# Nine norms of a two-block transformer kernel: one product with a matrix of ones, a square root and a reciprocal in place of column sums, a power and a spread

## The chip, the cores and the metric

The kernel runs on one core of a Trainium2 chip. Its engines go by short names here: PE is TensorE (PEld its weight loads), ACT is ScalarE, DVE is VectorE, POOL is GpSimd, SP is SyncE. The metric is the device time of one launch in microseconds (us).

## The reference, cut to what matters

One launch runs a conformer-like block over 256 tokens of 1024 features (in-projection, convolution and retention, out-projection, feed-forward, and a gated projection of a second input, "PLE"), and then two blocks of a transformer with conditioned norms (differential attention, then neighbourhood attention, each with a SwiGLU feed-forward), over 256 tokens and, in the first of the two, 256 context tokens. All of it is float32. What the change touches is the root-mean-square norm that stands at many places:

```python
def rmsnorm(x, w):
    xf = x.astype(jnp.float32)
    y = xf * lax.rsqrt(jnp.mean(xf * xf, axis=-1, keepdims=True) + EPS)
    return (y * w.astype(jnp.float32)).astype(x.dtype)

def first_block(...):
        ...
        x = x + rmsnorm(y, mix_post_norm[i])
        h = rmsnorm(x, ffn_pre_norm[i])
        f = (silu(h @ w_ffn_gate[i]) * (h @ w_ffn_up[i])) @ w_ffn_down[i]
        x = x + rmsnorm(f, ffn_post_norm[i])
        e = sigmoid(x @ w_ple_gate[i]) * (p[i] @ w_ple_proj[i])
        x = x + rmsnorm(e, ple_post_norm[i])

def second_block(...):
    for i in range(DEPTH_2):
        ...
        xn = modulate(rmsnorm_2(h, norm_mix[i]), sh_m, sc_m)
        ...
        h = h + g_m * y
        h = h + g_f * swiglu(modulate(rmsnorm_2(h, norm_ffn[i]), sh_f, sc_f), ...)
        if not last:
            hc = hc + cg_m * yc
            hc = hc + cg_f * swiglu(modulate(rmsnorm_2(hc, norm_ffn[i]), csh_f, csc_f), ...)
    return rmsnorm_2(h, norm_final)
```

## The kernel before

**Layout.** Activations are kept transposed: 8 tiles of 128 features by 256 tokens (`h[0..7]`, and `hc[0..7]` for the context). A norm over the features is therefore a sum over the 128 partitions of a tile and over the 8 tiles. Weights stream in through SP's queue as float32 blocks `raw`; ACT rounds each to a short-mantissa part `hi` (L132, a cast), DVE takes the rest `lo` (L133, a subtraction), and PE makes each float32 product of three short ones (L171, L172, L173, started 0.12 us apart at the full clock when nothing waits). Nearly all of PE's instructions are such triples, into the PSUM banks `mm`, `s` and `o`; the tiles of activations that they read are split the same way (`x`, by ACT at L154 or L670 and DVE at L155 or L671).

**A norm.** Class `Stat` gathers the squares. For each of the 8 tiles `add` lets ACT square it (L231 for the first, into `acc`; L234 for the others, into `sq`) and DVE add the square to `acc` (L236), save for the last square, which stays apart. `rstd` then makes the scale. For `acc` and for the last `sq`, two products each with a column of ones give the 256 sums as two columns of 128 (L247, four instructions, which the trace shows as 8 records). DVE scales them and adds EPS (L217), POOL raises them to the power -0.5 (L218), and two products with the identity spread each column over the partitions again, as 128 by 256 in a PSUM bank `t` (L256, 4 records). Then DVE multiplies tiles by that bank (L560 behind out_proj and the first block's feed-forward, L667 in the conditioned norms, L757 behind PLE, L1257 in the norm "NE" of the last feed-forward, where two columns are appended), or a copy of it is made first (L263, and L1288 at the end of the program). `fill` is a pair of hooks with which a norm puts other ready products behind the column products and behind the spreading ones, so that PE has work while DVE and POOL make the scale.

**Where norms stand.** There are 14, all made with that method. Nine are touched by the change; I number them by time: 1 behind out_proj (134 us), 2 behind the first block's feed-forward (358), 3 behind PLE (419), 4 and 5 behind the out-projection of differential attention, for `h` (621) and `hc` (642), 6 and 7 behind the first feed-forward of the transformer, for `h` and `hc` (990, 1015), 8 the norm NE (1210), 9 the final norm (1390). In the final norm the outputs are already multiplied by the norm's weights (L1281), and POOL (3 tiles, L1292) and DVE (5 tiles, L1295) multiply them by the scale and issue the transfers to the output.

**What sets the order.** Each engine runs its instructions in program order. That order is chosen when the kernel is built, by a scheduler that lays out the instructions of all engines by its own estimates, with hints in the code (`tc.issue_after(x)` places what follows behind `x`). So a change in one place can also move instructions of other lines.

**Functions of ACT.** Square root, exponential, tanh and SiLU need a table loaded into ACT, and a load (an instruction of its own, ACT_TABLE_LOAD) stands ahead of an activation whenever its function is not in the table that is loaded. The kernel before has 5 loads.

## Time and profile before

| | us |
|---|---|
| median of 3 runs (lowest, highest) | 1398.66 (1398.44, 1399.48) |
| the profiled execution, its own time | 1401.17 |
| its span (first to last instruction) | 1399.4 |
| PE busy in the span | 1368.7 (98%) |
| DVE busy | 1073.0 (77%) |
| ACT busy | 696.4 (50%) |
| POOL busy | 62.1 (4%) |
| mean granted clock of PE, as a share of the full one | 0.993 |

The page gives the busy time of each engine, the chain of work that ended last, and the costliest groups of instructions. A busy PE is one with an instruction under way; the end of each product is modelled, 0.28 us behind its start, while the next one starts 0.12 us behind it, so idle time of PE is read a little short: a gap of 0.51 us in a row is 0.67 us by the starts of the products around it. The other views are the timeline (start, length, engine, line, operation, and in square brackets how long the engine was idle before it and for whom), the groups by line, one line with those that waited for it, and busy times by stretch.

### The profile page before, as it was taken

How to read it: one execution, taken by the hardware profiler on the slowest of the kernel's cores; microseconds unless marked ns; L12 is line 12 of the kernel's file. 1: busy time of each engine (PE TensorE's matmuls, PEld its weight loads, DVE VectorE, ACT ScalarE, POOL GpSimd, SP SyncE). 2: the span in 40 equal slices, each digit the busy share in tenths (PEclk: the TensorE clock that was granted, in tenths of full speed). 3: DMA queues.
4: the chain of work that ended last, by engine and by line, in shares of the span. 5: the costliest groups of instructions: out<-in, count | busy, mean ns of one | idle time of the engine just before them, and what ended most of it. 6: DMA issues, size and time to landing. Idle time of an engine off the chain costs nothing.

```text
span 1399.4 us, 24793 instructions
## 1 busy us (share of the span) xinstructions
PE 1368.7 (98%) x9465; PEld 1231.3 (88%) x9465; DVE 1073.0 (77%) x2167; ACT 696.4 (50%) x1316; POOL 62.1 (4%) x119
## 2 busy tenths in 40 slices
PE   7999999999999999999999999999999999999997
PEld 7798799999999989899888888888998888888886
DVE  7975899986678878977799999964765467798764
ACT  6656544454465777655332222323545456655442
POOL 0001000000000222310000000000000000000000
PEclk9999999999999999999999999999999999999998
DMA  8456688767455333334565676644632234355463
GB/s 294 137 167 208 225 304 293 228 201 220 161 178 176 107 113 122 106 96 154 168 213 186 219 237 224 205 132 116 200 121 95 80 91 135 124 195 185 154 187 93
DMA packets 78600, 239.76 MB, mean 171 GB/s; under 512 B 8977, under 2 KB 14609, under 8 KB 78353
## 3 DMA queue, kind: packets, MB, share of 16 engines
q1 hardware_dynamic: 77760, 237.65, 52.6%
q8 instruction: 74, 1.21, 0.3%
q10 hardware_dynamic: 720, 0.53, 0.1%
q14 instruction: 46, 0.37, 0.1%
HBM read 237.10 MB, written 1.05 MB: 170 GB/s over the span
## 4 chain that ended last, share of the span: by engine, by line
PE 91%; DVE 3%; ACT 2%; issue 1%; POOL 1%; DMA 1%; SPq 0%; POOLq 0%; DVEq 0%; ACTq 0%
PE mm L171 20%; PE mm L172 19%; PE mm L173 19%; PE mm L183 5%; PE s L183 2%; PE mm L185 2%; PE mm L198 2%; PE mm L200 2%; PE mm L199 2%; PE s L821 1%; PE s L171 1%; PE t L852 1%; PE s L172 1%; PE s L173 1%; PE s L1131 1%
## 5 line engine op out<-in xcount | busy, mean ns | idle before, releaser
L132 ACT CAST hi<-raw 128x1024 fp32r<-128x1024 f32 (+3 forms) x383 | 364.7, 956 | 504.4 <-PE mm L172 261.5
L133 DVE TENSOR_TENSOR lo<-raw,hi 128x1024 fp32r<-128x1024 f32 (+3 forms) x383 | 422.0, 1104 | 149.8 <-ACT hi L132 146.9
L171 PE MATMUL mm<-x,hi 128*128 128x256 f32 (+2 forms) x1412 | 445.1, 317 | 9.2 <-ACT x L154 6.1
L172 PE MATMUL mm<-x,hi 128*128 128x256 f32 (+2 forms) x1412 | 443.0, 314 | 2.0 <-DVE x L155 1.1
L173 PE MATMUL mm<-x,lo 128*128 128x256 f32 (+2 forms) x1412 | 442.1, 314 | 1.8 <-DVE lo L133 1.8
L171 PEld LDWEIGHTS mm<-x,hi 128*128 128x128 f32 x1412 | 270.3, 192 | 39.4 <-issue 12.2
L172 PEld LDWEIGHTS mm<-x,hi 128*128 128x128 f32 x1412 | 271.4, 192 | 20.9 <-issue 3.3
L173 PEld LDWEIGHTS mm<-x,lo 128*128 128x128 f32 x1412 | 271.4, 192 | 19.4 <-issue 2.9
L292 DVE SCALAR_TENSOR_TENSOR junk<-adaw,sb 128x512 f32<-128x512 f32 x320 | 219.9, 687 | 12.6 <-DMA adaw<-ada 8.2
L173 PE MATMUL mm<-o,lo 128*128 128x256 f32 (+1 forms) x284 | 85.0, 301 | 0.0
L172 PE MATMUL mm<-o,hi 128*128 128x256 f32 (+1 forms) x284 | 84.5, 300 | 0.0
L171 PE MATMUL mm<-o,hi 128*128 128x256 f32 (+1 forms) x284 | 83.8, 302 | 0.6 <-ACT o L150 0.5
L218 POOL TENSOR_TENSOR rv<-rv,mhalf 128x2 f32<-128x2 f32 (+1 forms) x16 | 16.5, 1032 | 1185.2 <-DVE rv L217 1185.2
L198 PE MATMUL mm<-hi,x 128*128 128x256 f32 x240 | 68.7, 286 | 0.0
L199 PE MATMUL mm<-lo,x 128*128 128x256 f32 x240 | 68.6, 286 | 0.0
L200 PE MATMUL mm<-hi,x 128*128 128x256 f32 x240 | 68.6, 286 | 0.0
L172 PE MATMUL mm<-q,hi 128*128 128x256 f32 (+1 forms) x195 | 61.1, 313 | 0.0
L171 PE MATMUL mm<-q,hi 128*128 128x256 f32 (+1 forms) x195 | 61.0, 313 | 0.0
L173 PE MATMUL mm<-q,lo 128*128 128x256 f32 (+1 forms) x195 | 61.0, 313 | 0.0
L171 PEld LDWEIGHTS mm<-o,hi 128*128 128x128 f32 x284 | 53.5, 191 | 3.8 <-ACT o L150 0.9
L173 PEld LDWEIGHTS mm<-o,lo 128*128 128x128 f32 x284 | 54.2, 191 | 2.1 <-issue 0.4
L172 PEld LDWEIGHTS mm<-o,hi 128*128 128x128 f32 x284 | 54.2, 191 | 1.8
(301 smaller groups left out, 2408.2 us busy)
## 6 DMA issues: line engine op xcount, KB each, us to landing
raw<-gu SPq DMA_DIRECT2D x88, 512.0 KB, 4.3
adaw<-ada SPq DMA_DIRECT2D x80, 512.0 KB, 4.6
raw<-wqkv SPq DMA_DIRECT2D x72, 512.0 KB, 4.3
raw<-ffn SPq DMA_DIRECT2D x44, 512.0 KB, 5.1
raw<-down SPq DMA_DIRECT2D x37, 384.0 KB, 3.1
raw<-down SPq DMA_DIRECT2D x37, 320.0 KB, 3.0
raw<-w_in SPq DMA_DIRECT2D x22, 512.0 KB, 5.5
o<-ada SPq DMA_DIRECT2D x32, 256.0 KB, 5.2
```

Source lines behind the costliest of these rows:

```text
L132: last_conv[:] = [act.copy(hi[:, :n], raw[:, :n]).ins, dve.tensor_tensor(lo[:, :n], raw[:, :n], f32(hi[:, :n]), op=ALU.subtract).ins]
L133: dve.tensor_tensor(lo[:, :n], raw[:, :n], f32(hi[:, :n]), op=ALU.subtract).ins]
L171: pe.matmul(out, wh, xh, start=first and k == 0, stop=False)
L172: pe.matmul(out, wh, xl, start=False, stop=False)
L173: last_mm[0] = pe.matmul(out, wl, xh, start=False, stop=last and k == n - 1).ins
L183: last_mm[0] = pe.matmul(out, wh, x, start=first and k == 0, stop=end).ins
L185: last_mm[0] = pe.matmul(out[:, :T], wl, x[:, :T], start=False, stop=False).ins
L198: pe.matmul(out, xh[:, ts_], wh, start=first and k == 0, stop=False)
L199: pe.matmul(out, xh[:, ts_], wl, start=False, stop=False)
L200: last_mm[0] = pe.matmul(out, xl[:, ts_], wh, start=False, stop=last and k == n - 1).ins
L218: pool.tensor_tensor(out, out, mhalf[:, :n], op=ALU.pow)
L292: dve.scalar_tensor_tensor(out=junk, in0=raw[:, gs_], scalar=1.0, in1=sb[:, v, gs_], op0=ALU.mult, op1=ALU.mult, accum_out=acc[:, n, v, g: ...
```

## The change

Nine of the 14 norms get a flag `root`. In them

- the last square is added to `acc` by DVE too (L244 of the new numbering, one more L236), save in norm 9, which has the flag `apart` and keeps it apart;
- one product of a 128 by 128 matrix of ones with `acc` (L255, 128x256, in norm 9 two: `acc` and the last square) sums over the partitions and leaves the sum in every one of them; both `fill` hooks are put behind it;
- ACT takes the square root of the bank, with scale 1/1024 and bias EPS, into `acc` in SBUF (L260), and DVE takes the reciprocal in place, 128x256 (L261);
- the result is in SBUF, not in PSUM, and the copies at L263 (norm 8) and L1288 (norm 9) go;
- behind the seventh square an activation of one column (L242) makes the table load of the square root come there, and not at L260. Functions that come after it load their own table again: there are 14 loads where there were 5.

```diff
-        def __init__(self, n, of=1024):
-            self.n, self.of, self.acc, self.left = n, of, None, of // P
+        def __init__(self, n, of=1024, root=False, apart=False):
+            self.n, self.of, self.acc, self.left, self.root, self.apart = n, of, None, of // P, root, apart or not root
...
             self.last_sq = act.activation(sq[:, :n], src, AF.Square).ins
-            if self.left:
+            if self.root and self.left == 1:
+                with tc.issue_after(self.last_sq):
+                    act.activation(first, ones[:, 0:1], AF.Sqrt)
+            if self.left or not self.apart:
                 self.last_add = dve.tensor_tensor(self.acc[:, :n], self.acc[:, :n], sq[:, :n], op=ALU.add).ins
             else:
                 self.last = sq
...
             ps = bank(pst, "t")
+            if self.root:
+                srcs = (self.acc, self.last) if self.apart else (self.acc,)
+                for src in srcs:
+                    mm = pe.matmul(ps[:, :T], ones, src, start=src is srcs[0], stop=src is srcs[-1])
+                if fill:
+                    fill[0](mm.ins)
+                    fill[1](last_mm[0])
+                r = self.acc if r is None else r[:, :T]
+                act.activation(r, ps[:, :T], AF.Sqrt, scale=1.0 / self.of, bias=eps)
+                dve.reciprocal(r, r)
+                return r
...
-    st = Stat(T)
+    st = Stat(T, root=True, apart=True)
...
     r = st.rstd(keep=False)
-    rs = tmp1()
-    act.copy(rs, r[:, :T])
     for k in (5, 0, 6, 1, 7, 2, 3, 4):
         o = outs[k // 2][:, (k % 2) * T:(k % 2 + 1) * T]
         if k > 4:
-            pool.tensor_tensor(o, o, rs, op=ALU.mult)
+            pool.tensor_tensor(o, o, r, op=ALU.mult)
```

The lines of the kernel before that stand behind the added code have numbers that are 4 to 19 higher after: L236 is L244, L560 is L579, L587 is L606, L603 is L622, L667 and L671 are L686 and L690, L1005 is L1024, L1281 is L1300.

ACT's instructions at norm 1, where the squares read out_proj's banks (`mm`), L587 copies these banks out, the casts are weights of the feed-forward, and L603 copies products of PLE. Before:

```order
L234 ACTIVATE sq<-mm 128x256 x2
L587 ACTIVATE q<-mm,vec 128x256 x2
L234 ACTIVATE sq<-mm 128x256 x2
L587 ACTIVATE q<-mm,vec 128x256 x2
L132 CAST hi<-raw 128x1024 x3
L603 ACTIVATE pt<-s 128x512
L132 CAST hi<-raw 128x1024
L603 ACTIVATE pt<-s 128x512 x2
L154 ACTIVATE x<-h_85,vec 128x256
```

After:

```order
L238 ACTIVATE sq<-mm 128x256
L242 ACT_TABLE_LOAD
L242 ACTIVATE first<-ones 128x1
L238 ACTIVATE sq<-mm 128x256
L606 ACTIVATE q<-mm,vec 128x256 x2
L132 CAST hi<-raw 128x1024 x3
L622 ACTIVATE pt<-s 128x512
L260 ACTIVATE acc<-t,eps 128x256
L132 CAST hi<-raw 128x1024
L622 ACTIVATE pt<-s 128x512 x3
```

The load and its activation stand ahead of the last square, and the square root stands behind three casts and one copy.

DVE's instructions at norm 1, up to the first multiplications by the scale (L560, which is L579 after). Before:

```order
L236 TENSOR_TENSOR acc<-acc,sq 128x256 x3
L217 TENSOR_SCALAR rv<-t 128x2
L133 TENSOR_TENSOR lo<-raw,hi 128x1024 x2
L560 TENSOR_TENSOR t_1748<-q,t 128x256
L560 TENSOR_TENSOR t_1756<-q,t 128x256
L133 TENSOR_TENSOR lo<-raw,hi 128x1024
```

After:

```order
L133 TENSOR_TENSOR lo<-raw,hi 128x1024
L244 TENSOR_TENSOR acc<-acc,sq 128x256 x4
L133 TENSOR_TENSOR lo<-raw,hi 128x1024 x3
L261 RECIPROCAL acc<-acc 128x256
L133 TENSOR_TENSOR lo<-raw,hi 128x1024
L579 TENSOR_TENSOR t_1745<-q,acc 128x256
L579 TENSOR_TENSOR t_1753<-q,acc 128x256
```

Three additions became four, the scaling of the columns is gone, and three subtractions of weights stand ahead of the reciprocal, where none stood ahead of L217; from the additions to the first multiplication there are four where there were two.

DVE's instructions at norm 5, where L1005 (L1024) adds the projection to the context tiles, L667 and L671 (L686, L690) make the tiles of norm 4's output, and the last multiplications follow. Before:

```order
L1005 SCALAR_TENSOR_TENSOR hc_96<-s,mod_108,hc_96 128x256
L133 TENSOR_TENSOR lo<-raw,hi 128x1024
L667 SCALAR_TENSOR_TENSOR t_8313<-h_91,mod_108,t 128x256
L671 SCALAR_TENSOR_TENSOR x<-t_8301,mod_108,x 128x256
L133 TENSOR_TENSOR lo<-raw,hi 128x1024
L671 SCALAR_TENSOR_TENSOR x<-t_8305,mod_108,x 128x256
L671 SCALAR_TENSOR_TENSOR x<-t_8309,mod_108,x 128x256
L217 TENSOR_SCALAR rv<-t 128x2
L667 SCALAR_TENSOR_TENSOR t_8317<-h_92,mod_108,t 128x256
```

After:

```order
L690 SCALAR_TENSOR_TENSOR x<-t_8283,mod_110,x 128x256
L686 SCALAR_TENSOR_TENSOR t_8295<-h_91,mod_110,acc 128x256
L133 TENSOR_TENSOR lo<-raw,hi 128x1024
L690 SCALAR_TENSOR_TENSOR x<-t_8287,mod_110,x 128x256
L690 SCALAR_TENSOR_TENSOR x<-t_8291,mod_110,x 128x256
L686 SCALAR_TENSOR_TENSOR t_8299<-h_92,mod_110,acc 128x256
L244 TENSOR_TENSOR acc<-acc,sq 128x256
L690 SCALAR_TENSOR_TENSOR x<-t_8295,mod_110,x 128x256
L690 SCALAR_TENSOR_TENSOR x<-t_8299,mod_110,x 128x256
L261 RECIPROCAL acc<-acc 128x256
L686 SCALAR_TENSOR_TENSOR t_8515<-hc_93,mod_110,acc 128x256
```

The last square's addition (L244) stands four instructions ahead of the reciprocal, and PE's one product of norm 5 comes between the two; before, PE's products waited for the last square only, and L217 was what stood here. On PE that product stands where the column products stood, with the triples of the next weights behind it.

ACT's instructions at the end of the program. Before:

```order
L234 ACTIVATE sq<-h_91 128x256
L1281 ACTIVATE x<-h_91,vec 128x256
L234 ACTIVATE sq<-h_92 128x256
L1281 ACTIVATE x<-h_92,vec 128x256
L1288 COPY t_15860<-t 128x256
L1293 DMA out<-x 128x256 x3
```

After:

```order
L238 ACTIVATE sq<-h_91 128x256
L242 ACT_TABLE_LOAD
L242 ACTIVATE first<-ones 128x1
L1300 ACTIVATE x<-h_91,vec 128x256
L238 ACTIVATE sq<-h_92 128x256
L1300 ACTIVATE x<-h_92,vec 128x256
L260 ACTIVATE acc<-t,eps 128x256
L1310 DMA out<-x 128x256 x3
```

The load stands behind the square of the seventh tile (`h_91`), and the square root in the place of the copy.

## Rows read from the trace of the kernel before

**Rows 1.** the page: busy time by engine, chain that ended last, and one costly group

```profile
PE 1368.7 (98%) x9465; PEld 1231.3 (88%) x9465; DVE 1073.0 (77%) x2167; ACT 696.4 (50%) x1316; POOL 62.1 (4%) x119
...
PE 91%; DVE 3%; ACT 2%; issue 1%; POOL 1%; DMA 1%; SPq 0%; POOLq 0%; DVEq 0%; ACTq 0%
...
L133 DVE TENSOR_TENSOR lo<-raw,hi 128x1024 fp32r<-128x1024 f32 (+3 forms) x383 | 422.0, 1104 | 149.8 <-ACT hi L132 146.9
```

**Rows 2.** one source line, the power on POOL (L218), and who waited for it

```profile
L218 POOL TENSOR_TENSOR rv<-rv,mhalf x16: 693/697/2069, 23.1 to 1391.3; 128x2 f32<-128x2 f32 x14, 128x4 f32<-128x4 f32 x2
...
  PE t L256: 2.6, 4
```

**Rows 3.** timeline by start time, out_proj into post_norm: start, length, engine, line, operation [idle before]

```profile
134.29 0.50 PE L247 MATMUL t<-ones,acc 128*128 128x1 f32 x4
134.31 2.96 ACT L132 CAST hi<-raw 128x1024 fp32r<-128x1024 f32 x3
...
135.11 0.36 PE L171 MATMUL s<-x,hi 128*128 128x256 f32 x1
...
135.59 1.65 POOL L218 TENSOR_TENSOR rv<-rv,mhalf 128x2 f32<-128x2 f32 x1 [25.54 <-DVE rv L217]
...
137.29 0.71 PE L256 MATMUL t<-tab,rv 128*128 128x128 f32 x4 [0.51 <-POOL rv L218]
...
137.82 0.39 PE L171 MATMUL s<-x,hi 128*128 128x256 f32 x1
...
138.04 0.75 DVE L560 TENSOR_TENSOR t<-q,t 128x256 f32<-128x256 f32 x2 [0.22 <-PE t L256]
...
142.19 0.39 PE L172 MATMUL mm<-x,hi 128*128 128x256 f32 x1 [0.82 <-DVE x L155]
```

**Rows 4.** groups of VectorE by line and shape: busy us, mean ns of one | idle before

```profile
L236 DVE TENSOR_TENSOR acc<-acc,sq 128x256 f32<-128x256 f32 x80 | 33.3, 418 | 7.8 <-ACT sq L234 6.9
...
L836 DVE RECIPROCAL sc<-sc 128x1 f32<-128x1 f32 x16 | 2.5, 158 | 6.0 <-ACT e L831 6.0
...
L836 DVE RECIPROCAL sc<-sc 128x2 f32<-128x2 f32 x8 | 1.3, 160 | 3.8 <-ACT e L831 3.8
...
L779 DVE TENSOR_SCALAR nlam<-nlam 128x1 f32<-128x1 f32 x1 | 0.1, 148 | 0.0
```

**Rows 5.** the same view of ScalarE: a table load and a one-column activation

```profile
L1083 ACT ACT_TABLE_LOAD x1 | 1.3, 1283 | 0.0
...
L110 ACT ACTIVATE first<-ones 128x1 f32<-128x1 f32 x1 | 0.2, 203 | 0.0
```

**Rows 6.** timeline: the one product with ones of this shape, and the next start

```profile
87.33 0.60 PE L439 MATMUL t<-rp,ones 128*128 128x256 f32 x2
87.76 0.59 PE L503 MATMUL s<-q 128*128 128x256 f32 x2
```

**Rows 7.** timeline around the end of the second norm behind wo0

```profile
641.60 0.42 DVE L236 TENSOR_TENSOR acc<-acc,sq 128x256 f32<-128x256 f32 x1
...
643.36 0.61 PE L247 MATMUL t<-ones,sq 128*128 128x1 f32 x4 [0.63 <-ACT sq L234]
...
646.57 0.15 DVE L217 TENSOR_SCALAR rv<-t 128x2 f32<-128x2 f32 x1
```

**Rows 8.** busy time, granted clock (behind the engines), DMA share of a ten us stretch there

```profile
640.00:650.00 10.00, 9.17 (x63) 8.91 (x63) 8.58 (x20) 4.63 (x9) 0.69 (x1) 0.83 0.83 303
```

**Rows 9.** timeline at the start of the products behind the NE norm

```profile
1216.75 0.39 PE L171 MATMUL mm<-x,hi 128*128 128x258 f32 x1 [0.50 <-DVE t L1257]
```

**Rows 10.** timeline of the last norm

```profile
1390.31 0.60 PE L247 MATMUL t<-ones,sq 128*128 128x1 f32 x4 [0.74 <-ACT sq L234]
...
1392.01 0.96 PE L256 MATMUL t<-tab,rv 128*128 128x128 f32 x4 [1.10 <-POOL rv L218]
1393.01 0.37 ACT L1288 COPY t<-t 128x256 f32<-128x256 f32 x1 [2.35 <-PE t L256]
...
1393.45 2.09 POOL L1292 TENSOR_TENSOR x<-x,t 128x256 f32<-128x256 f32 x3 [1.50 <-ACT t L1288]
```

More of the change, by code (lines that the diff above doesn't have):

```diff
@@ L212, in body @@
     dve.memset(mhalf, -0.5)
+    eps = const.tile([P, 1], F32, name="eps")
+    dve.memset(eps, EPS)
     def inv_sqrt(out, src, scale):
```

12 lines of the change are left out of this document (6 added, 6 removed).

## The prediction, made before the changed kernel ran

> **What bounds the kernel now.** I read the page first: PE is busy 1368.7 us of a span of 1399.4 us, and the chain that ended last lies 91% on PE [rows 1]. So the time is PE's list of instructions plus the holes in it, and a change to the norms is worth two things: instructions that leave PE's list, and holes that close. ACT (50% busy) and DVE (77%) count where PE waits for them. The second view was the power on POOL: it took 693 ns at least, and PE waited for it 4 times, 2.6 us in all; at the other ten norms products that were ready covered it [rows 2]. I then looked at each of the nine norms in the timeline. They fall into four kinds. PE waits for the power at norms 1, 2 and 3 (0.51 us of idle time each) and at 9 (1.10). PE waits behind norm 8 for the first tile that was scaled (0.50) [rows 9]. At 4, 6 and 7 the list of PE has no hole. At 5, DVE is the late one.
>
> **PE's list.** At norm 1 the eight column products take from 134.29 to 135.11, 0.82 us, and the four spreading ones from 137.29 to 137.82, 0.53 [rows 3]. The one product that takes their place has its like in the trace: 128x256 with a matrix of ones, two records, 0.43 us from its start to the next product's start [rows 6]. That is 0.82 + 0.53 - 0.43 = 0.92 us less; part of the 0.53 is the start behind a wait, so I take 0.85. This is sure at each norm where PE is the bound and the product finds its operand ready.
>
> **The new chain.** Before, it ran from column products over L217, the power and the spreading products to DVE. After, it is one product, a square root, a reciprocal. The square root reads 128x256 from PSUM as the copy L1288 does, 0.37 us [rows 10]; I take 0.4. The reciprocal of 128x256 isn't in the trace. Its lower bound is the addition of 128x256, 418 ns; its upper bound comes from the narrow ones: a reciprocal of one column takes 158 ns, 10 more than a one-column scaling (148), and if all of that 10 were the price of one element, 256 would take 0.15 + 2.56 = 2.7 us [rows 4]. Between these ends stands the row with two columns, 160 ns: 2 ns more for one more element, at most 0.16 + 0.51 = 0.67 us for 256. It is nearest to the low end, and I take 0.42 us.
>
> The Trainium skill speaks against this. "VectorE: DVE Perf Modes" (First, the fixed hardware budget) says that a reciprocal runs as an iterated divide with a repeat count of 8. If that is 8 cycles for each element, my estimate from that page's 0.96 GHz is 256 x 8 / 0.96 = 2.1 us. The step from one to two columns, 2 ns where 8 cycles would be 8.3, speaks against that reading, which is why it is a rival and not the forecast.
>
> **Norm by norm**, against the profiled execution's own time, 1401.17 us:
>
> Norm 1. Here the change adds a wait. The last two squares read the same bank, and between them stand now the table load and its one-column activation, 1.28 + 0.20 = 1.5 us [rows 5]. The last square, which ended by 134.29, ends some 1.4 to 1.5 us later, its addition takes 0.42 more [rows 4], so PE's product, which stands where the column products stood, starts at about 135.7: a hole of about 1.4 us. On ACT the square root stands behind three casts that began at 134.31 and took 2.96 us [rows 3] and one copy of some 0.6; all of this moves 1.5 us later: 134.3 + 1.5 + 3.0 + 0.6 + 0.4, so it ends at about 139.8. The reciprocal follows, then a subtraction of weights (1.1 us in the mean [rows 1]), and the first multiplication, at 138.04 before [rows 3], comes at about 141.9, 3.8 us late. What is hidden: the products after it wait for tiles x from DVE and ACT anyway (0.82 us at 142.19 [rows 3], and more such waits behind it), so PE's hole counts only through these tiles; and two of the subtractions that stood between the later multiplications now stand ahead of them, 2 x 1.2 to 1.45 with what they wait for. I take 3.8 - 2.9 = +0.9 us. Ends: -1.5 if the tiles are not late, +2.7 if none of the reordering helps by more than one subtraction.
>
> Norms 2 and 3. The last square is done long before PE comes to the product (at neither does the profile show the column products waiting), so the load on ACT is covered by PE's products. PE's list is 0.85 shorter and the hole for the power, 0.51 idle or 0.67 by starts, has no cause any more: -1.5 us each. The scale is ready sooner also, since the power took 1.65 us where DVE worked beside it [rows 3].
>
> Norms 4 and 5. Norm 4 gives PE's 0.85. At norm 5, DVE is the bound: L217 ran at 646.57, 2.6 us behind the end of the products (643.36 + 0.61) [rows 7], with DVE busy 8.58 of 10 us and PE 9.17 [rows 8]. The two norms put two additions and two reciprocals on DVE and take two scalings off, 2 x (0.42 + 0.42 - 0.15) = 1.4 us [rows 4, 7], and what PE saves at norm 5 isn't reached there. Moreover PE's product must wait for the last addition in DVE's queue, and the triples of the next weights are queued behind it. Sum for both: -0.85 + 1.4 = +0.6 us. Ends: -1.7 if the new order of DVE hides its own additions, +3 if PE's product stands for the addition behind two subtractions. The granted clock is 0.83 in the mean here [rows 8], a part at the full level of 2.4 GHz and a part at the half, behind two holes of PE, the later one of 0.63 us [rows 7]; a hole that closes or opens can move such a part, which is in those ends.
>
> Norms 6 and 7. Ready products follow, more than thirty on PE ahead of the product itself: -0.85 each.
>
> Norm 8. -0.85, and the 0.50 us for the first scaled tile [rows 9], 0.66 by starts, goes, as the scale needs no copy and no power: -1.5.
>
> Norm 9. Nothing hides anything here, it is the end of the chain. Before: the last square's products start at 1390.31, and POOL's first multiplication starts at 1393.45 [rows 10], 3.14 us. After: product 0.43 and 0.2 to its landing, square root 0.4, reciprocal 0.42 with 0.1 of hand-overs: 1.6 us, so -1.55. Its table load comes behind the seventh square, ahead of the last matrix products: covered.
>
> Sum: +0.9 - 1.5 - 1.5 + 0.6 - 0.85 - 0.85 - 1.5 - 1.55 = -6.2 us. The profiled execution would go from 1401.17 to 1394.9; the median of the runs shown lies 2.5 us lower, and I apply the same step there: 1398.66 - 6.2 = 1392.5 us. One term I set to zero with bounds of 2 us on both sides: the order of the attention heads between 440 and 620 us is laid out anew by the scheduler.
>
> **The rivals.** *The reciprocal is slow.* At 2.2 us, in the upper part of the stretch from 0.42 to 2.7, it adds 1.8 us wherever its result is awaited: norm 1 +1.8, norm 2 +1.4 (its tiles have some slack), norm 3 +0.7, norm 5 +1.4, norm 8 +0.7, norm 9 +1.8, together +7.8. The kernel then takes 1398.66 - 6.2 + 7.8 = 1400.3, no change that can be told. For: the 10 ns that one column takes above a scaling. Against: the step of 2 ns to the second column [rows 4]. Chance 0.14.
>
> *The table loads stand on the chain: slower.* There are 9 more loads with their activation, 1.49 us each [rows 5], and ACT feeds the casts of every weight. If ACT were awaited at each, 9 x 1.49 = 13.4 us come on top of the -6.2, 1405.9 us. It decides from 6 of the 9 on (9.0 us), where the kernel is slower by 0.2%. For: norm 1, where the load delays PE by all of its length. Against: ACT is busy half of the time, and at L1083 the load is followed by its activation with 0.0 us idle before it [rows 5]. Chance 0.10. The Trainium skill, "ScalarE: Activation LUTs" (What ACT_TABLE_LOAD costs; Table sets: the hidden batching unit), warns of just this pattern: it gives about 2.66 us for each switch, with a drain behind the load, and asks to batch by table. The rows agree on the load, 1283 ns, and show no drain. By its price and nine exposed switches the sum would be 24 us more, an estimate from that page.
>
> *The gain in the middle is given back.* If the supply of weights paces PE between the norms, a shorter list of PE only lengthens the next wait, and the ends at norms 8 and 9 alone remain: -3 us, 1395.6, on the border of what can be told. Against: the waits of PE for DMA do not show at these places. Chance 0.10, half of it within 0.2%.
>
> **How the numbers follow.** A measurement of this kernel can tell about 0.2%, 2.8 us, from no change. The forecast has 0.66, all of it faster; the slow reciprocal 0.14, of which 0.11 within 0.2% and 0.03 slower; the loads 0.10 slower; the gain given back 0.10, half and half. Faster 0.66 + 0.05 = 0.71; same 0.11 + 0.05 = 0.16; slower 0.13. The forecast's own range is -6.2 with norm 1 from -1.5 to +2.7, norms 4 and 5 from -1.7 to +3, and the heads 2 both ways: most of it between 1388.5 and 1396.5. To leave out no more than 2 in 10 the range has to reach the slow reciprocal: 1388.5 to 1400.5.
>
> **What would show it.** The row of L261 decides the first rival: 0.4 us or over 2. PE's product L255 at norm 1 should begin 1.4 us behind the triples before it; at norms 2, 3 and 9 no product should wait for POOL. The POOL multiplication at the end should start 1.6 us behind the last square. PE busy should fall by 6 to 8 us and ACT's rise by 12 to 15. I am wrong if PE shows new idle time ahead of casts (`hi`) behind the loads, or if a stretch of half the clock appears behind norm 1's hole.

## The result: 1.04% slower, and the profile after

The changed kernel takes 1412.77 us (median of 4 runs, 1412.41 to 1414.08), the kernel before 1398.55 in the same comparison; the ratio is 1.0104, 95% interval 1.0091 to 1.0117. That is +14.2 us where -6.2 was forecast, and 12 us beyond the upper end of the range. The profiled execution took 1413.06 us with a span of 1411.3.

The page of the changed kernel, busy time by engine and the chain that ended last:

```profile
PE 1365.2 (97%) x9377; PEld 1226.5 (87%) x9377; DVE 1092.2 (77%) x2176; ACT 713.7 (51%) x1341; POOL 52.1 (4%) x110
...
PE 91%; DVE 4%; ACT 2%; issue 1%; DMA 1%; POOL 0%; DVEq 0%; SPq 0%; ACTq 0%
```

Against [rows 1]: PE is busy 3.5 us less, DVE 19.2 and ACT 17.3 us more, and PE holds the same 91% of the chain. PE's idle time in the span rose from 30.7 to 46.1 us. So PE's list did become shorter, and the loss lies in holes of PE and, as the clock below shows, in products that ran at half the speed and count as busy. The groups of DVE by line and shape (busy us, mean ns of one | idle before):

```profile
L261 DVE RECIPROCAL acc<-acc 128x256 f32<-128x256 f32 x8 | 14.0, 1748 | 3.7 <-ACT acc L260 3.7
...
L855 DVE RECIPROCAL sc<-sc 128x2 f32<-128x2 f32 x8 | 1.3, 163 | 3.6 <-ACT e L850 3.6
```

The reciprocal of 128x256 takes 1.75 us. The two-column one, the row on which the forecast leaned [rows 4], still takes 0.16.

The waits of PE over the whole changed kernel, the longest kinds (what waited and for what: us in total, times, longest us):

```profile
PE mm L171 <- ACT x L154: 8.6, 3, 5.5
PE mm L172 <- DVE x L690: 3.7, 2, 2.4
PE s L840 <- ACT o L150: 2.4, 1, 2.4
PE mm L171 <- DVE t L1276: 2.4, 1, 2.4
PE mm L171 <- ACT x L689: 2.2, 1, 2.2
...
PE s L171 <- ACT pt L622: 1.4, 1, 1.4
PE t L255 <- DVE acc L244: 1.4, 1, 1.4
```

The wait for POOL [rows 2] is gone at the changed norms. In its place stand waits for tiles that are scaled (x, t): norm 5 (3.7 us, L690, in two waits of 2.4 and 1.3), norm 8 (2.4, L1276), norms 6 and 7 (2.2, L689), norm 1 (2.1 for x at L154, where 5.5 of the row's 8.6 are at the program's start, as 5.2 were before; 1.4 for the copies L622, 1.4 for the one product's own operand), and one at the first heads of attention (2.4, L840).

The second thing that the profile shows is the clock. Busy times in stretches of the changed kernel (stretch, its length, busy us and count of PE, PEld, DVE, ACT and POOL, granted clock, DMA share, GB/s):

```profile
146.00:149.40 3.40, 3.40 (x18) 3.40 (x18) 3.15 (x10) 1.53 (x5) 0.00 (x0) 0.50 0.36 133
446.30:449.70 3.40, 3.40 (x15) 2.75 (x16) 1.33 (x3) 3.06 (x6) 0.43 (x2) 0.50 0.77 272
576.00:582.80 6.80, 6.14 (x26) 5.14 (x27) 6.34 (x20) 2.33 (x6) 0.51 (x2) 0.50 0.48 148
647.70:654.50 6.80, 5.49 (x23) 5.31 (x24) 5.58 (x10) 1.39 (x4) 0.00 (x0) 0.50 0.50 169
1030.00:1033.40 3.40, 3.40 (x19) 3.40 (x18) 3.40 (x10) 1.71 (x4) 0.00 (x0) 0.50 0.00 0
1228.00:1231.40 3.40, 3.40 (x18) 3.40 (x17) 3.40 (x9) 2.33 (x6) 0.00 (x0) 0.50 0.56 196
```

and of the kernel before:

```profile
399.00:402.40 3.40, 3.40 (x19) 3.40 (x18) 0.64 (x2) 1.53 (x2) 0.62 (x1) 0.51 0.26 95
573.10:576.50 3.40, 3.33 (x13) 2.58 (x14) 3.40 (x12) 1.21 (x5) 2.02 (x3) 0.50 0.66 202
644.80:648.20 3.40, 3.40 (x18) 3.40 (x18) 3.19 (x7) 0.58 (x2) 0.69 (x1) 0.50 0.82 260
1030.00:1033.40 3.40, 3.40 (x31) 3.40 (x30) 1.82 (x2) 1.94 (x3) 0.00 (x0) 1.00 0.00 0
```

At each of these places PE is granted 0.50, the level of 1.2 GHz. Between 67 us and the last norm the kernel before has three such stretches, 10.2 us, the changed kernel six, of which two are of double length, 27.2 us. The fourth row of before lies at the full clock: 31 products in 3.4 us, where the fifth of after has 19. What PE did before the clock fell: it had waited 2.1 us for x at norm 1 (until 143.64, the clock falls at 146.0), 2.4 at the first heads (445.20, 446.3), 0.9 and 1.9 at a later one (573.47 and 576.66, 576.0), 2.4 at norm 5 (647.08, 647.7, with 1.3 more inside the stretch), 2.2 at norm 7 (1027.71, 1030.0), 2.4 at norm 8 (1226.63, 1228.0). The same hole is not always followed by such a stretch: 1.33 us of idle time until 1191.12 in the kernel before is not, and 1.32 at the same place in the trace of e4 (until 1189.35, the clock falls at 1191.2) is; 2.06 at the heads is in e2 (until 456.07) and not in e3 (until 450.60), with PE's order the same.

**Where the time went, by stage.** The 383 weight casts (L132) stand in the same order in all the kernels, so the time between the starts of two of them is a stage that can be compared. (Products of PE can change sides at such a boundary: in the changed kernel and in e5 eight of them, about 1 us, are made in the stage of the heads instead of that of norms 4 and 5, in e14 fourteen.) The boundary casts of the kernel before start at 66.6 and 184.8 us (norm 1), 335.9 and 367.6 (norm 2), 394.8 (the unchanged norm ahead of PLE), 424.3 (norm 3), 595.5 (heads of attention), 694.9 (norms 4 and 5), 973.8 and 1053.0 (6 and 7), 1182.9 and 1251.0 (8), and 1379.5 for the stretch to the end (9). Each number is the stage of that kernel minus the stage of the kernel before, in us, from the one profiled execution of each; the stages left out between them differ by 0.2 at most, and the stretch ahead of 66.6 us, where nothing is changed, by -1.6 (e3 and e7) to +3.6 (e1). One execution can lie far from its kernel's median: that of e3 is its fastest, those of e10 and e14 their slowest.

| kernel | 1 | 2 | ahead of PLE | 3 | heads | 4, 5 | 6, 7 | 8 | 9 |
|---|---|---|---|---|---|---|---|---|---|
| forecast | +0.9 | -1.5 | 0 | -1.5 | 0 | +0.6 | -1.7 | -1.5 | -1.55 |
| changed kernel | +3.2 | -1.7 | +1.2 | -3.2 | +7.9 | -0.3 | +3.2 | +2.4 | +0.3 |
| e1, no loads | +1.7 | -1.7 | +1.2 | -3.2 | +7.2 | -1.2 | +3.2 | +2.3 | +0.3 |
| e2, fast operation | +1.4 | -1.7 | +0.7 | -0.6 | +3.7 | +0.4 | -1.8 | +4.0 | -1.0 |
| e3, both | -0.1 | -1.7 | +0.7 | -2.9 | +0.7 | +0.3 | -1.8 | +2.0 | -1.0 |
| e10, one activation | +1.9 | -1.7 | +0.7 | -0.6 | +0.7 | +0.4 | -1.8 | +3.6 | -1.5 |
| e7, norm 1 alone | +3.1 | 0 | 0 | 0 | -0.1 | 0 | 0 | -0.5 | -0.2 |
| e5, norm 3 alone | 0 | 0 | 0 | -1.3 | +7.4 | -2.2 | +0.3 | -0.5 | +0.2 |
| e6, norms 6, 7 alone | 0 | 0 | 0 | -1.5 | -0.7 | 0 | +3.2 | -0.5 | -0.3 |
| e8, norm 8 alone | 0 | 0 | 0 | -1.5 | -0.7 | -1.0 | 0 | +4.9 | -0.2 |
| e11, norms 2, 6, 7, 9, one activation | 0 | -1.7 | +0.7 | -1.5 | -0.7 | +0.1 | -1.8 | +1.0 | -1.5 |

What a number of 1 to 2 us in a stage that a kernel doesn't change is, is mostly the clock. In the stage of norm 3, executions of the same instructions are 1.5 us shorter where they miss the 3.4 us at half clock that the kernel before has there (e6, e8, e11); in that of norm 8 one has them and is at +1.2 (the kernel with norm 9 alone), others have none and are at -0.5, so 1.7 us. Behind wo0 it is 1.0, in the heads 0.1 to 1.2. The changed kernel has 17 us more at half clock than the kernel before, five stretches: one more at each of norm 1, norms 4 and 5, 6 and 7, and 8, two more in the heads, one less at norm 3. At those prices, with 1.7 at norms 1, 6 and 7, that is an estimated 5 of the 13.0 us in its row; at half of their length, what PE's half speed takes where nothing else is waited for, it is 8.5. The heads come out by the second price: PE is idle there 4.4 us more than before, and half of the 6.8 us more at half clock is 3.4, together 7.8 of the 7.9. The runs give a figure between the two. Among the runs of one kernel 0.001 of the mean granted clock goes with 1.06 us (a fit to all the runs of this case), and the changed kernel's runs lie at 0.988, those of the kernel before at a median of 0.995 beside e1 to e4: an estimated 7.4 of the 14.2 us go with the clock.

The profiled execution of before lies 2.6 us over its median, that of after 0.3; so 11.9 of the 14.2 us are in the traces, and the rest fits that the kernel before usually had a little less of the slow clock than in its trace (the median of its runs is 0.994 or 0.995 in the comparisons that list it, the trace shows 0.993). The table's numbers for norm 3, the heads and norms 4 and 5 are low by as much as the three stretches in that trace cost.

### The profile page after: what moved, and what is told of

Its sections match the earlier page's. It is cut to its first block, busy times and chain, and to the rows that moved or that the text cites. A ratio compares the mean times of both kernels' runs of the same rounds, so it can differ in the third digit from the quotient of the medians.

```text
span 1411.3 us, 24634 instructions
## 1 busy us (share of the span) xinstructions
PE 1365.2 (97%) x9377; PEld 1226.5 (87%) x9377; DVE 1092.2 (77%) x2176; ACT 713.7 (51%) x1341; POOL 52.1 (4%) x110
## 4 chain that ended last, share of the span: by engine, by line
PE 91%; DVE 4%; ACT 2%; issue 1%; DMA 1%; POOL 0%; DVEq 0%; SPq 0%; ACTq 0%
PE mm L171 20%; PE mm L172 20%; PE mm L173 19%; PE mm L183 5%; PE s L183 2%; PE mm L185 2%; PE mm L198 2%; PE mm L200 2%; PE mm L199 2%; PE s L840 2%; PE s L171 1%; PE s L172 1%; PE s L173 1%; DVE lo L133 1%; PE t L871 1%; PE s L1150 1%
## 5 line engine op out<-in xcount | busy, mean ns | idle before, releaser
L132 ACT CAST hi<-raw 128x1024 fp32r<-128x1024 f32 (+3 forms) x383 | 364.5, 956 | 493.6 <-PE mm L172 253.7
L198 PE MATMUL mm<-hi,x 128*128 128x256 f32 x240 | 69.4, 289 | 0.8 <-DVE q L155 0.8
L171 PE MATMUL s<-x,hi 128*128 128x256 f32 (+1 forms) x176 | 50.6, 290 | 1.5 <-ACT pt L622 1.4
```

Of the source, the lines that this page charges most:

```text
L132: last_conv[:] = [act.copy(hi[:, :n], raw[:, :n]).ins, dve.tensor_tensor(lo[:, :n], raw[:, :n], f32(hi[:, :n]), op=ALU.subtract).ins]
L171: pe.matmul(out, wh, xh, start=first and k == 0, stop=False)
L198: pe.matmul(out, xh[:, ts_], wh, start=first and k == 0, stop=False)
```

## The experiments

**e1: no table loads.** PE's and DVE's instructions stand in the changed kernel's order.

```diff
-                    act.activation(first, ones[:, 0:1], AF.Sqrt)
+                    act.activation(first, ones[:, 0:1], AF.Square)
...
-                act.activation(r, ps[:, :T], AF.Sqrt, scale=1.0 / self.of, bias=eps)
+                act.activation(r, ps[:, :T], AF.Identity, scale=1.0 / self.of, bias=eps)
```

> The changed kernel with the table taken out: the root at L260 becomes an identity with the same scale and bias, and the one-column activation a square, so that no norm needs a load and none is made again after it. The scale is left wrong (the mean square's reciprocal, without the root). PE's and DVE's instructions and their order are those of the changed kernel; ACT has 9 loads fewer. Theory A (the reciprocal of 1.75 us, 1.33 more than forecast, wherever its result is awaited, is most of the 14 us): the time stays near the changed kernel's 1412.8, down by 2 to 3 us at norm 1 alone, where the load delays the last square: 1410 to 1411. Theory B (the loads hold ACT up, and with it the casts of the weights): 9 loads of 1.28 us, most of them gone from the chain: 1401 to 1404.

Measured: 1414.58 us (1410.67 to 1415.45), ratio 1.0112 (1.0095 to 1.0128): no gain that can be told. By stage the loads cost 1.5 us at norm 1 (+3.2 to +1.7) and 0.7 and 0.9 in two later ones, together 3.1, and in each of the three e1 has 3.4 us less at half clock; this kernel's trace lost 5.0 us more than the changed kernel's ahead of the first stage, where nothing is changed. So with the slow reciprocal in place the loads alone are not the cause. Theory B falls.

**e2 and e3: a fast operation in the place of the reciprocal**, with the loads and without.

```diff
+    one2 = const.tile([P, T], F32, name="one2")
+    dve.memset(one2, 1.0)
...
-                dve.reciprocal(r, r)
+                dve.tensor_tensor(r, r, one2, op=ALU.min)
```

> The changed kernel with the reciprocal replaced by a minimum with a tile of ones, 128x256, which should take about 0.42 us as the additions do; the scale is left out of the result that way. Root and loads stay. Since the order is laid out by the scheduler, instructions move too. Theory A: 1.33 us less at each norm where the scale is awaited, and the waits at the attention heads may go or stay: 1401 to 1405. Theory B: the loads are still there, 1409 to 1412. If the time falls below the kernel before (1398.6), the whole of the forecast but the reciprocal was right.

Measured: 1406.44 us (1403.56 to 1407.0), ratio 1.0055 (1.004 to 1.007): between the two theories, nearer to A.

> Both at once: minimum with ones in place of the reciprocal, identity in place of the root, no loads of the root's table. What is left is the chain that the forecast had in mind: one product, one activation, one operation of DVE at 0.42 us. By the forecast's terms, without the 0.9 us that the load cost at norm 1: 1392 to 1393. If it stays above the kernel before, 1398.6, the price lies in the new order of the instructions (theory C), not in the reciprocal or the loads.

Measured: 1399.78 us (1395.95 to 1402.4, 10 runs), ratio 1.0007 (0.9995 to 1.0019). So without reciprocal and loads no loss is left that could be told: some 6 us go with the reciprocal, and 7 with the loads once it is fast. The 6 us are not its time alone, since from the changed kernel to e2 the scheduler also moved instructions (PE's lists differ at 1053 of 9377 places); between e2 and e3 the orders of PE and DVE are the same. Nor are the 7 us a price of the loads by themselves: e10 below has all 14 loads and no operation on DVE, and loses some 1 us. In the traces of e2 and e3 most of the difference is the clock: from norm 1 to norm 8 e2 has 17 us more at half clock, and PE's idle time differs by some 1.5 us. That the loads were worth almost nothing in e1 fits that ACT's lateness counts only where DVE isn't later still; no run tests that. What the forecast called the sum without surprises, 1392 to 1393, didn't come: the trace of e3, its best run, shows -3.8 us in its stages, and the median is that of the kernel before. So the gain of 6 us is missing even without the two costs; theory C, the new order, fits that and was not tested by itself.

**e4: norm 9 alone.** The kernel before with `st = Stat(T, root=True, apart=True)` at the end and without the copy of the scale (L1288).

> The kernel before with the final norm alone changed; three instructions of PE, DVE and ACT differ, nothing else moves. Forecast with the reciprocal at 1.75 instead of 0.42 us: -1.55 + 1.33 = -0.2 us, 1398.3. If the table load ahead of it were in the way, +1.3 us.

Measured: 1400.66 us (10 runs, 1398.35 to 1404.54), ratio 1.0018 (1.0009 to 1.0027). The stage is +0.3 us: the price of a reciprocal that is hidden by nothing eats the gain. The timeline of the changed kernel shows it best (start, length, engine, line, operation):

```profile
1401.88 0.70 PE L255 MATMUL t<-sq,ones 128*128 128x256 f32 x2 [0.65 <-ACT sq L238]
1402.62 0.47 ACT L260 ACTIVATE acc<-t,eps 128x256 f32<-128x256 f32 x1 [0.39 <-PE t L255]
1403.13 1.75 DVE L261 RECIPROCAL acc<-acc 128x256 f32<-128x256 f32 x1 [1.80 <-ACT acc L260]
1404.91 3.35 DVE L1312 TENSOR_TENSOR x<-x,acc 128x256 f32<-128x256 f32 x5
1405.03 2.62 POOL L1309 TENSOR_TENSOR x<-x,acc 128x256 f32<-128x256 f32 x3 [788.94 <-DVE acc L261]
```

and of the kernel before:

```profile
1393.41 1.74 DVE L1295 TENSOR_TENSOR x<-x,t 128x256 f32<-128x256 f32 x5 [2.23 <-ACT t L1288]
```

From the product to POOL's multiplication it takes 3.15 us, as the 3.14 before [rows 10], 1.75 of them the reciprocal. The 0.3 us come behind that: from POOL's start to the end it takes 6.25 us where it took 5.93. DVE's five multiplications take 3.35 us for 1.74, and POOL's three 2.62 for 2.09 [rows 10]. Before, DVE read the scale from the PSUM bank and POOL from a copy in SBUF; now both read it from SBUF. All eight kernels with norm 9 changed show this, and none of the others; that the place of the scale is the reason was not tested. The table load is not in the way: it ends at 1395.91, the last square starts at 1401.42. The other 2 us of the median aren't in the stages of e4's trace, which is 0.3 us shorter than that of before, itself 2.6 over its median; part of them fits the clock (a mean of 0.994 in its ten runs, 0.995 in those of before), the rest stays open.

**e5 to e8: one norm changed, the rest as before.** They ask whether the losses are local.

```diff
-    st = Stat(T)
+    st = Stat(T, root=True)
```

(For norms 6 and 7 it is a pair of such objects, for norm 8 a list of one.)

> The kernel before with norm 3 (behind PLE) alone changed. In the changed kernel the stage around norm 3 is 3.2 us shorter than before and the attention heads behind it are 7.9 us longer. Theory A (the scheduler's new order of the heads comes from norm 3, and it leaves PE waiting at the first heads): both appear here, -3.2 + 7.9 = +4.7, 1403.4. Theory B (the heads suffer from what norms 1 and 2 moved, or from norms 4 and 5 behind them): norm 3 alone is a gain of about 3 us, 1395.5, and the heads take their former time.

> The kernel before with norms 6 and 7 alone changed. With a reciprocal of 1.75 us on DVE and fewer ready products ahead of the context's tiles (19 for 41), PE waits there as in the changed kernel, 2.2 and 0.8 us, and a stretch of half the clock follows. Theory A (local): +3.2 us at this stage, nothing elsewhere, 1401.9. Theory B (it needs the table loads or the other norms): between -1.7 and 0, 1397 to 1398.7.

> The kernel before with norm 1 alone changed. Theory A (local: the load ahead of the last square makes a hole of 1.4 us before the one product, the reciprocal comes behind three subtractions, and a stretch of half the clock follows): +3.2 us at this stage, 1401.9. Theory B (the three terms are made good by the slack of the tiles behind): 0 to +0.9, 1398.7 to 1399.6.

> The kernel before with the NE norm alone changed. Theory A (the reciprocal stands behind two subtractions on DVE and two more stand behind it, so the first scaled tile is late, PE waits about 2.4 us instead of 0.5, and a stretch of half the clock follows): +2.4 us at this stage, 1401.1. Theory B (the price there is made by the heads of neighbourhood attention ahead of it, whose order the other norms moved): -1.5 to 0, 1397.2 to 1398.7.

Measured: norm 3 alone 1403.94 us, ratio 1.0035 (1.0022 to 1.0049); norms 6 and 7 alone 1403.35, 1.0031 (1.002 to 1.0042); norm 1 alone 1402.33, 1.0027 (1.0014 to 1.0039); norm 8 alone 1402.74, 1.0024 (1.0011 to 1.0036). By the table the losses are local: +3.1 at norm 1 as in the changed kernel (+3.2), +3.2 at norms 6 and 7 (+3.2), and the 7.4 us at the heads come with norm 3 alone (7.9). Norm 8 alone is at +4.9 instead of +2.4, with one more stretch of half the clock in the trace; it begins at 1189.8, ahead of the changed instructions. Theory A held in all four, by the stages; the medians lie 0.4 to 1.6 us over its totals. The waits of PE with norms 6 and 7 alone, around the stage:

```profile
PE mm L171 <- ACT x L689: 2.2, 1, 2.2
PE mm L198 <- DVE q L155: 0.8, 1, 0.8
```

are the 2.2 and 0.8 us of the changed kernel.

**e9: reciprocals of nine widths**, the first of DVE's work, on a tile that nothing else reads.

```diff
+    probe = const.tile([P, 256], F32, name="probe")
+    dve.memset(probe, 1.0)
+    for w in (1, 2, 4, 8, 16, 32, 64, 128, 256):
+        dve.reciprocal(probe[:, :w], probe[:, :w])
+    for w in (8, 64, 256):
+        dve.tensor_tensor(probe[:, :w], probe[:, :w], probe[:, :w], op=ALU.mult)
```

> The kernel before with nine reciprocals of a tile of ones added on DVE at the start, 1, 2, 4, 8, 16, 32, 64, 128 and 256 columns wide, and three multiplications (8, 64 and 256 columns), among DVE's first instructions; nothing reads them. The forecast took the step from one column to two (2 ns) for the price of a column; 256 columns took 1746 ns. Theory A: a column costs (1746 - 160) / 255 = 6.2 ns from some width on, and the narrow ones hide it behind a fixed time of some 150 ns: 8 columns near 200 ns, 64 near 550, 128 near 950. Theory B: the price is a step at a certain width, not a price for each column.

The groups of DVE by line and shape, those of the added code (busy us, mean ns of one):

```profile
L216 DVE RECIPROCAL probe<-probe 128x256 f32<-128x256 f32 x1 | 1.7, 1746 | 0.0
...
L216 DVE RECIPROCAL probe<-probe 128x128 f32<-128x128 f32 x1 | 0.9, 946 | 0.0
...
L216 DVE RECIPROCAL probe<-probe 128x64 f32<-128x64 f32 x1 | 0.5, 546 | 0.0
...
L218 DVE TENSOR_TENSOR probe<-probe 128x256 f32<-128x256 f32 x1 | 0.4, 418 | 0.0
...
L216 DVE RECIPROCAL probe<-probe 128x32 f32<-128x32 f32 x1 | 0.4, 353 | 0.0
...
L218 DVE TENSOR_TENSOR probe<-probe 128x64 f32<-128x64 f32 x1 | 0.2, 221 | 0.0
...
L216 DVE RECIPROCAL probe<-probe 128x8 f32<-128x8 f32 x1 | 0.2, 203 | 0.0
L216 DVE RECIPROCAL probe<-probe 128x4 f32<-128x4 f32 x1 | 0.2, 178 | 0.0
L216 DVE RECIPROCAL probe<-probe 128x2 f32<-128x2 f32 x1 | 0.2, 166 | 0.0
...
L216 DVE RECIPROCAL probe<-probe 128x1 f32<-128x1 f32 x1 | 0.1, 128 | 0.0
```

Theory A. From two columns on every column costs the same: 178 - 166 = 12 ns for two, (353 - 203) / 24 = 6.25 for one, (1746 - 946) / 128 = 6.25. A column of the multiplication costs a sixth of that: (418 - 221) / 192 = 1.03 ns. The one execution took 1400.69 us, as the kernel before does (median 1400.46).

**e10: one activation.** ACT's function of the reciprocal square root of the absolute value makes the scale in one step, and DVE does nothing.

```diff
-                    act.activation(first, ones[:, 0:1], AF.Sqrt)
+                    act.activation(first, ones[:, 0:1], AF.Abs_reciprocal_sqrt)
...
-                act.activation(r, ps[:, :T], AF.Sqrt, scale=1.0 / self.of, bias=eps)
-                dve.reciprocal(r, r)
+                act.activation(r, ps[:, :T], AF.Abs_reciprocal_sqrt, scale=1.0 / self.of, bias=eps)
```

> The changed kernel with ACT's function of the reciprocal square root (of the absolute value) in place of the square root, and no reciprocal on DVE: the scale is ready 0.47 us after the product, DVE gets no extra work, and a table load stands in each norm as before. Theory A (reciprocal and loads both cost, the first more): less than with the fast operation on DVE (1406.4), 1402 to 1405, and above the kernel without loads (1399.8). Theory B (the new order alone costs): as with the fast operation, 1406.

Measured: 1401.78 us (10 runs), beside 1400.46 of the kernel before in the same comparison, ratio 1.0008 (0.9999 to 1.0017): nothing of the loss is left that could be told. Theory B falls; theory A was right in its direction, and its 1402 to 1405, for a kernel before at 1398.6, was still too much. The group of that activation:

```profile
L260 ACT ACTIVATE acc<-t,eps 128x256 f32<-128x256 f32 x8 | 3.8, 476 | 3.2 <-PE t L255 3.0
```

It takes as long as the square root did (0.47 us), and all 14 loads are there, so the difference to the changed kernel is the reciprocal, and the order that was laid out around it. The heads are at +0.7 and norms 6 and 7 at -1.8.

**e11 and e12: the same in some norms only**, those whose stage was shorter in e2 by 1 us and more (2, 6, 7, 9), and with 4 and 5 as well.

> As the run before, but in norms 2, 6, 7 and 9 alone, the stages that were shorter than before with the fast operation on DVE and the loads in place: -1.7 at norm 2, -1.8 at 6 and 7, -1.0 at 9. If the stages add up as the runs with one norm did: 1398.7 - 4.5 = 1394.2. If the reordered parts cost elsewhere, about 1398.7.

> The same with norms 4 and 5 as well, whose stage was +0.4 us with the fast operation and -0.3 in the changed kernel, mostly by the clock. With the reciprocal's 2 x 1.75 us off DVE, which was the late engine there: -0.85 to -1.7 more than the run before, 1392.5 to 1393.4; if the load in the middle of the casts holds DVE up there, +1.5 more, 1395.7.

Measured: 1396.81 us (11 runs), ratio 0.998 (0.9972 to 0.9989), and 1397.33 us, ratio 0.9978 (0.9969 to 0.9988), beside 1400.46 of the kernel before in the same comparison. Both are faster than both kernels, by 0.2%, not by the 4.5 us and more that the stages promised: of norm 2's 1.7 us, 0.7 are given back in the stage behind it. Norms 4 and 5 add nothing that can be told.

**e13: norm 3 alone, with the one activation.** In e5 two things moved at the heads.

> Norm 3 alone changed, with the one activation in place of square root and reciprocal (one table load ahead, as with the root). With root and reciprocal norm 3 alone cost 7.4 us at the attention heads and gave 1.3 at its own stage. Theory A (the reciprocal on DVE, which the scheduler answers with another order of the first heads): without it the heads lose at most 1 us, and the total is 1397 to 1399. Theory B (the move of the exponential's table load into the first head, which is the same in both): the heads lose the same 7 us, 1403 to 1404.

Measured: 1400.55 us (10 runs), ratio 1.0007 (0.9998 to 1.0016). The heads are at +2.1 instead of +7.4, the stage ahead at -2.7. The waits of PE in the stretch of the heads, with the reciprocal (e5):

```profile
PE s L840 <- ACT o L150: 2.4, 1, 2.4
PE t L871 <- ACT pt L864: 2.0, 3, 0.9
PE t L862 <- DVE e L859: 1.9, 1, 1.9
```

and with the one activation:

```profile
PE s L839 <- ACT e L849: 2.5, 5, 1.0
PE t L870 <- ACT pt L863: 2.4, 3, 1.4
...
PE s L839 <- ACT o L150: 1.2, 1, 1.2
```

So the total is near theory A's, and most of the loss goes with the reciprocal. The holes don't: PE is idle in the heads 4.4 us more than in the kernel before in e5, and 4.0 in e13. With the reciprocal one of the waits is 2.4 us long, with the one activation none is over 1.4, and the trace has 10.2 us at half clock in the heads where that of e13 has 3.4, as the kernel before; half of the difference is 3.4 of the 5.3 us. The mean granted clock of the runs differs too (0.992 in e5, 0.994 in e13). Whether the long wait comes from the reciprocal's time on DVE just ahead of the first heads or from the other order that the scheduler laid out can't be told apart, since one goes with the other.

**e14 and e15: norm 2 alone, and norms 4 and 5 alone.**

> The kernel before with norm 2 alone changed, square root and reciprocal as in the changed kernel. There PE has ready products to do while the scale is made, and its stage was 1.7 us shorter in every kernel: 1397.0. If the reciprocal's 1.3 us beyond the forecast is paid in the tiles behind it, -0.3 and 1398.4.

> The kernel before with norms 4 and 5 alone changed. By the forecast DVE, the late engine there, gets two additions and two reciprocals: with 1.75 us each +0.6 + 2 x 1.33 = +3.3, 1402.0. By the changed kernel's own stage, -0.3 us, which had one stretch of half the clock more: -2, 1396.7.

Measured: norm 2 alone 1403.51 us (5 runs, 1399.47 to 1406.45), ratio 1.0032 (1.0014 to 1.0051); norms 4 and 5 alone 1400.43 (10 runs), ratio 1.0015 (1.0002 to 1.0029). By stage norm 2 is -1.7 as everywhere, and +1.2 in the stage behind it; then come +1.2 at the heads, into which 14 products moved from the stage behind wo0, and +2.0 there, with 6.8 us at half clock instead of 3.4. Neither of the two expected totals came. So a kernel that is 0.5 us shorter at the changed place came out 4 us longer. That the clock's stretches fall otherwise is seen; why they do is open. Norms 4 and 5 are at +0.8, near the forecast's +0.6, not at +3.3.

The seven kernels with one place changed (e4 to e8, e14, e15) lose 25 us in sum by their medians, the changed kernel 14.2. So each of them loses some us that belong to no norm; the runs don't show why.

## Why the prediction was wrong, step by step

**The step that failed first: the reciprocal at 0.42 us.** The prediction bounded it by 0.42 and 2.7 and chose the low end, because the two-column row lay 2 ns above the one-column row. It takes 1.75 us. Means of 8 and 16 readings that lie between 147 and 166 ns can't carry a step of 2 ns, and e9 shows the true step beside them: 6.25 ns from two columns on. The truth lies between the bounds, and the slow reading was in kind the right one. The Trainium skill's page "VectorE: DVE Perf Modes" (First, the fixed hardware budget) said that a reciprocal repeats its divide; the trace agrees that a column costs several times that of a multiplication, and in size 6.25 ns is 6 cycles, an estimate by that page's 0.96 GHz, where a count of 8 would give 8.3 ns.

**But the slow reciprocal was a rival, priced at +1.6 us, and the result is +14.2.** That rival's step that failed is its list of places: it paid 0.7 to 1.8 us at six norms and nothing at 6 and 7, where "ready products follow". Too few of them followed. In the trace 20 of PE's products stand between the one product and the next block of weights (L198), the last two of which wait for the scaled tiles; before, 41 stood between the sums and that block. The timeline of DVE there:

```profile
1023.90 1.75 DVE L261 RECIPROCAL acc<-acc 128x256 f32<-128x256 f32 x1 [0.67 <-ACT acc L260]
1025.57 1.16 DVE L133 TENSOR_TENSOR lo<-raw,hi 128x1024 fp32r<-128x1024 f32 x1
1026.64 1.66 DVE L686 SCALAR_TENSOR_TENSOR t<-hc,mod,acc 128x256 f32<-128x256 f32 x4
```

From the reciprocal's start to the first multiplication 2.7 us pass, 1.75 in the reciprocal and 1.1 in a subtraction of weights behind it, and PE waits 2.2 us and once more 0.8. Forecast -1.7, measured +3.2; with a fast operation (e2, e3) and with none (e10) -1.8. The term was right for the kernel that it assumed.

**No price was set on a hole beyond its own length.** The prediction named the clock as a thing that would make it wrong, and gave it no time in the sum. Behind the long holes at norms 1, 5, 7 and 8 and at the heads PE was granted 0.50 for 3.4 us or 6.8, and 3.4 us of it cost 1.5 to 1.7 us where PE is the bound. At norms 6 and 7 the sum closes: 2.2 + 0.8 + 1.7 = 4.7 of the 5.0 us between -1.8 and +3.2. By the estimates above the clock is a third to over a half of the whole loss. Not every such hole is followed by the slow clock, so a part of this price is chance.

**Norm 1**: +0.9 forecast, +3.2 measured. The hole ahead of the one product was forecast at 1.4 us (1.38 measured). The timeline of the changed kernel:

```profile
134.52 0.67 PE L255 MATMUL t<-acc,ones 128*128 128x256 f32 x2 [1.38 <-DVE acc L244]
135.61 3.50 DVE L133 TENSOR_TENSOR lo<-raw,hi 128x1024 fp32r<-128x1024 f32 x3 [1.24 <-ACT hi L132]
...
137.85 0.49 ACT L260 ACTIVATE acc<-t,eps 128x256 f32<-128x256 f32 x1
...
139.03 1.74 DVE L261 RECIPROCAL acc<-acc 128x256 f32<-128x256 f32 x1
...
141.77 0.74 DVE L579 TENSOR_TENSOR t<-q,acc 128x256 f32<-128x256 f32 x2
...
143.64 0.62 PE L171 MATMUL mm<-x,hi 128*128 128x256 f32 x3 [2.11 <-ACT x L154]
```

The first multiplication at 141.77 looks like the forecast's 141.9, by luck. The changed kernel runs 1.3 us ahead here (its cast for the boundary at 66.6 starts at 65.3), so on the scale of the kernel before it is 143.1, 1.2 late; and the forecast's own terms, 139.8 + 0.42 + 1.1, give 141.3. The square root ended as forecast (138.34, which is 139.7). The reciprocal then began 0.7 us later, behind the third subtraction ahead of it on DVE, which the forecast had left out of the chain, and took 1.74. The offset was wrong too: the two subtractions that the new order had moved ahead were to give back 2.9 of the 3.8 us, but x came 2.1 us late. And a wait was overlooked, 1.4 us for the copies L622: both fills now stand behind one product, and the third fill needs a bank that ACT, behind its three casts, hasn't copied yet. The load is not the reason: without it the wait is still 1.2 us (e1 and e3). e1 and e2 share it out: 1.5 us for the load, with which the stretch at half clock goes too, and 1.8 for the reciprocal; without both (e3) the stage is at -0.1.

**Norm 2**: -1.5 forecast, -1.7 at the stage, of which 1.2 come back before the next norm (0.7 with a fast operation). **Norm 3**: -1.5 forecast, -3.2 in the trace with one half-clock stretch less (1.5), so about -1.7: right. **The heads**: 0 with bounds of 2 us, measured +7.9, 4.7 with norm 3's stage: 4.4 us more of PE's idle time and 6.8 more at half clock. That the new order is a matter of norm 3 was not seen, although the heads follow it on the same engines. **Norms 4 and 5**: +0.6 forecast, -0.3 and +0.8 (e15) measured: right in size, by luck in part. With the reciprocal's true time the forecast's own terms give +3.3, and the stage is at +0.4 without any reciprocal (e2, e10), so DVE's time counts for less there than the forecast took. **Norm 8**: -1.5 forecast, +2.4 measured. DVE's timeline says why:

```profile
1219.92 2.36 DVE L133 TENSOR_TENSOR lo<-raw,hi 128x1024 fp32r<-128x1024 f32 x2 [2.86 <-ACT hi L132]
1222.19 1.75 DVE L261 RECIPROCAL q<-q 128x256 f32<-128x256 f32 x1
1223.86 2.29 DVE L133 TENSOR_TENSOR lo<-raw,hi 128x1024 fp32r<-128x1024 f32 x2
1226.06 0.42 DVE L1276 TENSOR_TENSOR t<-mm,q 128x258 f32<-128x258 f32 x1
```

The reciprocal stands between four subtractions; the first scaled tile (L1276) is made at 1226.06, and PE, which waited 0.50 us for it before [rows 9], waits 2.4. The forecast counted the hole as closed because copy and power go, and looked at neither the reciprocal's length nor the four subtractions in DVE's queue. Without the reciprocal (e3, e10) the stage is still at +2.0 and +3.6, of which one and two stretches of half the clock, 1.7 and 3.4, are in the traces; so the -1.5 didn't come there either. **Norm 9**: -1.55 forecast, with 1.33 more for the reciprocal -0.2, measured +0.3; with an operation of 0.42 us in its place, which is the chain that the forecast had meant, -1.0 (e2 and e3), and -1.5 with one activation (e10), where that operation is gone too. The forecast stopped at POOL's first multiplication and left out that the last ones take longer, 0.3 us to the end.

**The loads** were a rival at 0.10, "slower" by an exposed 1.49 us at each of nine norms. They cost 1.5 us at norm 1, as said, and little elsewhere while the reciprocal was slow (e1); with a fast operation in its place they are some 7 us (e2 to e3), and with no operation on DVE some 1 us is left for them and all else (e10, at most 2.4 by the interval). The rival was weighed as if it stood alone. Of the drain that the Trainium skill's page "ScalarE: Activation LUTs" (What ACT_TABLE_LOAD costs) gives behind a load no run here shows a row.

**The signs.** L261 took neither 0.4 us nor over 2. No product waits for POOL at norms 2, 3 and 9, as forecast. POOL's multiplication at the end starts 3.2 us behind the last square, not 1.6. PE's busy time fell by 3.5 us, not 6 to 8, with 17 us more at half clock between 67 us and the last norm; ACT's rose by 17.3, not 12 to 15, which leaves out the nine square roots of 0.47. PE has no new idle time ahead of casts (`hi`; 0.7 us where there were 1.3), and a stretch of half the clock did appear behind norm 1's hole, the one sign of being wrong that came.

## What to carry to other kernels

Price an operation that the trace lacks by its rate per element, and don't take that rate from two narrow instructions that the fixed time hides: where bounds lie a factor of six apart and the likely end rests on 2 ns, the forecast is a coin. A helper that is used at nine places multiplies such an error by nine, and where an order is laid out anew, cover that hid a wait before has to be counted again, in the new order, for every place. A hole of some 2 us in a packed PE can cost more than itself, by the clock behind it: here 1.5 to 1.7 us where the stretch came.

## What the runs showed of the hardware that was not expected

- A reciprocal on DVE costs 6.25 ns for each column from two columns on (166 ns for 2, 1746 for 256), six times a column of a multiplication (221 ns for 64, 418 for 256: 1.03 each).
- One activation of the reciprocal square root took 0.47 us for 128x256 and stood in for a square root of the same length and 1.75 us of DVE.
- Executions of the same instructions, in stages that a kernel leaves alone, differ by up to 1.7 us with a 3.4 us stretch at a granted clock of 0.50, and runs of one kernel lie up to 7.4 us apart (1395.82 to 1403.23, the kernel before beside e5 to e8); the intervals of ten runs are 0.1% wide to each side.
- At the end of the program, beside POOL's multiplications, three of DVE's five multiplications of 128x256 by the scale took 0.94 us each where they had taken 0.41, and POOL's 0.90 instead of 0.72, once both engines read the scale from SBUF.
